# The first norm of a hybrid trunk: squares summed on TensorE, root spread by transpositions, first products in another order

## The chip, the cores and the metric

The kernel runs on one core of a Trainium2 chip. The metric is the device time of one execution in microseconds (us); the smaller the better. A core has TensorE (PE in the profile; PEld are its weight loads), VectorE (DVE), ScalarE (ACT), GpSimd (POOL) and SyncE (SP), which issues most of the loads. The four compute engines run their own instructions in order, and wait for each other by semaphores.

## The reference

The kernel computes two layers of a decoder trunk on one sequence of 1024 positions with 1024 channels. What matters here is the beginning: the first norm, its scale and shift, which come from the vector c, and the first product of the convolution module.

```python
def rms_norm(x, g):
    xf = x.astype(jnp.float32)
    y = xf * lax.rsqrt(jnp.mean(xf * xf, axis=-1, keepdims=True) + EPS)
    return (y * g.astype(jnp.float32)).astype(x.dtype)

def modulate(h, shift, scale):
    return h * (1.0 + scale[:, None, :]) + shift[:, None, :]

def reference(x, c, ada_w, ada_b, norm_mix_g, ...):
    c_act = jax.nn.silu(c)
    for i in range(DEPTH):
        mod = c_act @ ada_w[i] + ada_b[i]
        sh_m, sc_m, g_m, sh_f, sc_f, g_f = jnp.split(mod, N_ADA, axis=-1)
        h = modulate(rms_norm(x, norm_mix_g[i]), sh_m, sc_m)
        if i % N_MIXERS == 0:
            y = conformer_conv(h, ...)
        else:
            y = multiscale_pool(h, ...)
        x = x + (1.0 + g_m)[:, None, :] * y
        h = modulate(rms_norm(x, norm_ffn_g[i]), sh_f, sc_f)
        x = x + (1.0 + g_f)[:, None, :] * swiglu_ffn(h, ...)
    return rms_norm(x, final_g)
```

In the first layer `sh_m` and `sc_m` are dots of silu(c) with columns of `ada_w`; `conformer_conv` begins with `h @ w1`.

## The kernel before

Channels lie on the 128 partitions, positions along the free dimension. So x has eight channel tiles (KT = 8), and the sequence is worked in two chunks of 512 positions, A and B. All that the change touches is the opening for chunk A, the code of `trunk` from where `spread_c` is made to where the early weights of the next part are loaded, and `load_weight`.

The opening goes like this. SP issues loads in a fixed order (`load_next`): four transfers of x, each with two channel tiles, then `vecs` (all the small vectors), and then for each channel tile k a matrix `adaw` (two blocks of 128x1024: those rows of `ada_w` that give the shift and the scale of the tile's channels) and a weight `raw` (128x1024, the part of w1 for this channel tile and the first 2 x FIRST = 8 output tiles). TensorE spreads c over all partitions (the products named `c`), and ScalarE takes its SiLU (`cact`).

Of each channel tile the squares are taken, on VectorE for those in ON_DVE and on ScalarE for the others, and VectorE adds them up in `acc`. TensorE sums `acc` over the partitions: `mean_rsqrt` makes four products with `acc`'s 128x128 blocks as stationary operand and a column of `ones` (each 1/1024) as the moving one, into a bank named `var`. The function `rsqrt` takes the inverse root on VectorE in eight small operations on 128x4 elements (`col`, `var`). TensorE then spreads `col` over the partitions into the bank `rstd`, with `ident` as moving operand.

The loop over k (KT + 1 passes) then has, for each channel tile: two dots (`ada_dot`, a SCALAR_TENSOR_TENSOR of 128x1024 on VectorE that writes a column of `mod`), two small operations that make scale (`gains`) and shift (`mod`), then `t` = x times scale times rstd on VectorE, the high part of h on ScalarE (`h<-t,mod`), its low part on VectorE (`h<-t,mod,h`), and 24 products on TensorE: for each of the eight output tiles q (banks `first`), weight high x h high, weight high x h low, weight low x h high. A weight's high part is a CAST on ScalarE (`w<-raw`), its low part a subtraction (`w<-raw,w`), on VectorE for the first two (`own`) and on GpSimd for the others.

The order of TensorE's instructions is that of the code. On the other engines a scheduler chooses it from its own model of the times, bound by the manual dependences (`tc.add_manual_dep`), which keep an instruction behind another one of the same engine. After the opening the products `a` and `g` of the next output tiles begin, and pieces of work for VectorE and GpSimd are put beside them by a clock of planned costs.

The lines that set the order around the change are these:

```python
    ada_dot(w[:, 1], 0, 1, 0)
    tc.add_manual_dep(V_.last.ins, summed, edge, reason="behind the sums")
    rstd_p = now(mean_rsqrt(acc, A.n))
...
            for q in range(2 * FIRST):
                products(fb[q], wt, q, h_a[k - 1], k == 1, k == KT)
```

## Time and profile before

| | us |
|---|---|
| median of three runs | 1695.77 |
| lowest, highest | 1695.59, 1695.80 |
| the profiled execution | 1696.16 |
| its span, from the first to the last instruction | 1694.4 |
| TensorE busy in it | 1665.3 |
| VectorE busy in it | 1319.9 |

The profile is of one execution. Its page gives the busy time of each engine, the span in forty slices, the DMA queues, the chain of work that ended last and the costliest groups of instructions. Beside the page, the trace answers views of stretches: a timeline of instructions (start, length, engine, line, operation, output<-inputs, count, and in brackets the idle time before it with what ended it), groups by tile, and windows with busy time by engine. Names have no buffer numbers there. L149 and L126 are the lines of the helpers that issue a product and a vector operation, so one goes by the tiles' names. The whole opening lasts from 0 to 66 us of the span.

### The profile page before, as it was taken

The page shows a single profiled execution, that of the slowest core. Times are in us where ns is not written, and L with a number is a line of the kernel's source. Part 1 is how long each engine was busy: PE and PEld are TensorE (multiplying, and loading weights), DVE is VectorE, ACT ScalarE, POOL GpSimd, SP SyncE. Part 2 cuts the span into 40 slices and gives each one's busy share as a digit, 9 for nine tenths or more (in the row PEclk, how much of TensorE's full clock was granted, in tenths as well). Part 3 has the DMA queues.
Part 4 walks back from the last instruction along what each step waited for, and adds up shares of the span by engine and source line. Part 5 has one row for each costly group of instructions (what it writes and reads, how often), then busy time and mean ns, then how long its engine had stood idle before and what let it go on. Part 6 is the DMA issues. An engine that isn't in the chain of part 4 may idle for free.

```text
span 1694.4 us, 21271 instructions
## 1 busy us (share of the span) xinstructions
PE 1665.3 (98%) x7586; PEld 1356.4 (80%) x7586; DVE 1319.9 (78%) x1872; ACT 799.4 (47%) x1085; POOL 486.3 (29%) x566
## 2 busy tenths in 40 slices
PE   7999999999999999999999999999999999999997
PEld 5777777778887888888888888888888888888886
DVE  8889899899758887887665797848777677668657
ACT  3669686866546332333213336646422222234454
POOL 3587767796001111212110222100111111000013
PEclk9999999999999999999999999999999999999999
DMA  8858987828675788886878846877677776586564
GB/s 302 288 172 230 228 237 199 223 79 238 216 240 152 256 261 298 281 259 212 339 267 281 256 149 202 240 245 212 176 233 230 212 222 193 200 273 204 193 166 122
DMA packets 115820, 380.70 MB, mean 225 GB/s; under 512 B 12225, under 2 KB 14401, under 8 KB 115714
## 3 DMA queue, kind: packets, MB, share of 16 engines
q1 hardware_dynamic: 77888, 247.46, 41.3%
q0 software_dynamic: 36736, 130.83, 31.6%
q8 instruction: 60, 0.98, 0.2%
q10 hardware_dynamic: 1090, 1.05, 0.2%
q14 instruction: 46, 0.38, 0.1%
HBM read 311.92 MB, written 63.18 MB: 221 GB/s over the span
## 4 chain that ended last, share of the span: by engine, by line
PE 88%; DVE 5%; DMA 2%; ACT 2%; issue 2%; POOL 1%; DVEq 0%; SPq 0%; ACTq 0%; POOLq 0%
PE a L149 24%; PE dn L149 23%; PE e L149 13%; PE p L149 12%; PE y L149 6%; PE g L149 3%; PE first L149 3%; PE tap L149 2%; POOL pa L126 1%; PE ada L149 1%; DMA adaw<-in_adan_dram 1%; DVE t L126 1%; DVE x L126 1%; PE var L149 1%; DVE ca L126 0%
## 5 line engine op out<-in xcount | busy, mean ns | idle before, releaser
L126 ACT CAST w<-raw 128x1024 fp32r<-128x1024 f32 (+1 forms) x249 | 258.5, 1041 | 332.6 <-PE dn L149 98.6
L149 PE MATMUL dn<-g,w 128*128 128x512 f32 x1152 | 265.4, 391 | 2.3 <-DVE g L126 1.0
L149 PEld LDWEIGHTS dn<-g,w 128*128 128x128 f32 x1152 | 215.4, 188 | 48.7 <-DVE x L126 1.7
L126 DVE TENSOR_TENSOR w<-raw,w 128x1024 fp32r<-128x1024 f32 (+1 forms) x177 | 217.9, 1234 | 41.3 <-ACT w L126 40.8
L149 PE MATMUL a<-n,w 128*128 128x512 f32 x1056 | 247.7, 390 | 1.1 <-DVE n L126 0.7
L149 PE MATMUL p<-h,w 128*128 128x512 f32 x1056 | 244.2, 391 | 0.8 <-DVE h L126 0.6
L126 POOL TENSOR_TENSOR pa<-pa,pr 128x512 f32<-128x512 f32 x160 | 228.2, 1510 | 23.9 <-ACT pr L126 17.8
L149 PEld LDWEIGHTS a<-n,w 128*128 128x128 f32 x1056 | 197.9, 188 | 44.1 <-DVE n L126 2.2
L149 PEld LDWEIGHTS p<-h,w 128*128 128x128 f32 x1056 | 197.4, 188 | 43.7 <-DVE h L126 1.5
L149 PE MATMUL dn<-hi,w 128*128 128x512 f32 (+1 forms) x600 | 173.6, 373 | 0.4 <-DVE w L126 0.4
L126 DVE SCALAR_TENSOR_TENSOR ca<-u,vecs,ca 128x512 f32<-128x512 f32 x245 | 169.9, 748 | 0.5
L126 DVE SCALAR_TENSOR_TENSOR x<-dn,gains,x 128x512 f32<-128x512 f32 (+1 forms) x144 | 100.9, 732 | 35.9 <-PE dn L149 35.9
L149 PEld LDWEIGHTS dn<-hi,w 128*128 128x128 f32 x600 | 109.7, 188 | 20.4 <-DVE w L126 0.9
L149 PE MATMUL a<-t,w 128*128 128x512 f32 x528 | 123.6, 390 | 0.8 <-DVE w L126 0.8
L149 PE MATMUL e<-b,w 128*128 128x512 f32 x528 | 123.4, 389 | 0.6 <-DVE r L126 0.6
L149 PE MATMUL e<-t,w 128*128 128x512 f32 x528 | 123.2, 389 | 0.0
L126 ACT ACTIVATE pr<-u,vecs 128x512 f32<-128x512 f32 x160 | 108.3, 716 | 25.2 <-POOL pa L126 17.6
L1117 POOL DMA_DIRECT2D raw<-in_wgu_dram x41 | 36.3, 884 | 283.9 <-DVE k L126 100.7
L149 PEld LDWEIGHTS a<-t,w 128*128 128x128 f32 x528 | 99.1, 188 | 21.7 <-DVE w L126 1.2
L149 PEld LDWEIGHTS e<-b,w 128*128 128x128 f32 x528 | 99.1, 188 | 21.5 <-DVE r L126 1.1
L149 PEld LDWEIGHTS e<-t,w 128*128 128x128 f32 x528 | 99.2, 188 | 20.5
L149 PE MATMUL dn<-lo,w 128*128 128x512 f32 (+1 forms) x300 | 111.7, 372 | 0.0
(183 smaller groups left out, 2375.2 us busy)
## 6 DMA issues: line engine op xcount, KB each, us to landing
raw<-in_wgu_dram SPq DMA_DIRECT2D x132, 512.0 KB, 4.9
adaw<-in_ada_dram POOLq DMA_DIRECT2D x48, 512.0 KB, 7.4
raw<-in_wdn_dram SPq DMA_DIRECT2D x44, 512.0 KB, 7.9
raw<-in_wgu_dram POOLq DMA_DIRECT2D x41, 512.0 KB, 7.1
raw<-in_w_dram SPq DMA_DIRECT2D x36, 512.0 KB, 6.1
gd<-g POOLq DMA_DIRECT2D x36, 512.0 KB, 7.8
g<-gd SPq DMA_DIRECT2D x36, 512.0 KB, 5.8
kinds<-k POOLq DMA_DIRECT2D x33, 512.0 KB, 7.2
```

Source lines behind the costliest of these rows:

```text
L126: self.last = self.order(getattr(self.eng, name)(out, *args, **kw))
L149: last_mm[0] = nc.tensor.matmul(out, lhsT, rhs, start=start, stop=stop, skip_group_check=more).ins.name
L1117: d = order(nc.gpsimd.dma_start(w[i], wgu[l, fp, src], accum_op=ADD))
```

## The change

The squares are no longer added on VectorE. TensorE takes each of them as it comes: nine groups of four products into the bank `first_var`, the first with a constant tile `eps`, and the others with the squares of the eight channel tiles. Squares alternate between ScalarE and VectorE (ON_DVE is now 1, 3, 5, 7). The inverse root is taken as before, and `col` is spread by four transpositions (`turned`) in place of four products. The first matrix is loaded in two halves, the scale's half ahead of `vecs`; both of its dots stand behind the root. In the first channel tile the eight products of high with high parts come first, then those with h's low part, and then those with the weight's low part. The low parts of the first two weights stand behind t on VectorE, and the casts of the first four weights behind the previous h on ScalarE (`behind`). The SiLU of c's columns stands behind the last square.

```diff
--- before.py
+++ after.py
@@ -54,7 +54,7 @@
 DIAGS = 8
 LOAD = {"load": 4.0, "slow": 6.0, "next": 4.0, "dots": 4.0}
 
-ON_DVE = (1, 4)
+ON_DVE = (1, 3, 5, 7)
 AHEAD = 4
 RECENT = 6
 STRASSEN = (False, True)
@@ -362,6 +362,8 @@
     ones = cst.tile([P, P], F32, name="ones")
     V_.memset(ones, 1.0 / D)
     S_.activation(tmp.tile([P, 16], F32, tag="col0", name="first_act", bufs=1)[:, 0:1], ones[:, 0:1], AF.Silu)
+    eps = cst.tile([P, P], F32, name="eps")
+    V_.memset(eps, EPS_SUM)
     ident = cst.tile([P, P], F32, name="ident")
     make_identity(nc, ident)
     recip = cst.tile([P, PHALO], F32, name="recip")
@@ -485,12 +487,14 @@
         return mod[:, b : b + 1]
 
 
-    def load_weight(src, n=D, load=nc.sync.dma_start, summed=False, own=False):
+    def load_weight(src, n=D, load=nc.sync.dma_start, summed=False, own=False, behind=None):
         raw = raws.tile([P, D], F32, tag="raw", name=nm("raw"))[:, :n]
         dst = raw if len(src.shape) == 2 else raw.rearrange("p (a b) -> p a b", a=src.shape[1])
         load(dst, src)
         wt = wts.tile([P, 2, D], F32R, tag="w", name=nm("w"))
         S_.copy(wt[:, 0, :n], raw)
+        if behind:
+            tc.add_manual_dep(S_.last.ins, behind, edge, reason="behind the values before")
         if summed:
             S_.activation(wt[:, 1, :n], raw, AF.Copy, scale=-1.0)
             low = wt[:, 1, :n]
@@ -1680,49 +1684,58 @@
     spread_c = [bank("c") for _ in range(2)]
     for h in range(2):
         matmul(spread_c[h], ones[0:1, :], crow[:, h * 512 : h * 512 + 512], start=True, stop=True)
+    ada_m = ada.rearrange("(l j k) p d -> l k p j d", l=DEPTH, j=6)
+    first_w = wts.tile([P, 2, D], F32, tag="w", name=nm("adaw"))
+    load_next(first_w[:, 1], ada_m[0, 0][:, 1, :])
     load_next(vecs, vec)
-
-    squares = []
-
-    def square(k):
-        sq = temp(A.n) if k else temp(A.n, "acc", 2)
+    load_next(first_w[:, 0], ada_m[0, 0][:, 0, :])
+
+    first_var = bank("var")
+
+    def add_to_var(parts, first=False, last=False):
+        for i, part in enumerate(parts):
+            matmul(first_var[:, i : i + 1], part, ones[:, 0:1], start=first and i == 0, stop=last, more=True)
+
+    add_to_var([eps] * (A.n // P), True)
+    for k in range(KT):
+        sq = temp(A.n)
         if k in ON_DVE:
             V_.tensor_tensor(sq, x[0][k], x[0][k], op=MUL)
         else:
             S_.activation(sq, x[0][k], AF.Square)
-        squares.append(sq)
-
-    for k in range(KT):
-        square(k)
+            last_square = S_.last.ins.name
         if k == 2:
             for h in range(2):
                 S_.activation(cact[:, h * 512 : h * 512 + 512], spread_c[h], AF.Silu, scale=float(D))
-        if k > 1:
-            acc = squares[0]
-            V_.tensor_tensor(acc, acc, squares[k - 1], op=ADD)
-    V_.scalar_tensor_tensor(acc, squares[KT - 1], EPS_SUM, acc, op0=ADD, op1=ADD)
-    summed = V_.last.ins.name
+        add_to_var([sq[:, i * P : i * P + P] for i in range(A.n // P)], False, k == KT - 1)
     S_.activation(ccols[:, :, 0], V("c", 0, KT), AF.Silu)
     silu = S_.last.ins.name
+    tc.add_manual_dep(S_.last.ins, last_square, edge, reason="behind the squares")
     S_.activation(tmp.tile([P, 16], F32, tag="col0", name="second_act", bufs=1)[:, 0:1], ones[:, 0:1], AF.Sigmoid)
     tc.add_manual_dep(S_.last.ins, silu, edge, reason="the sigmoid's table early")
     scale_b = cst.tile([P, KT], F32, name="scale_b")
     G_.tensor_scalar(scale_b, V("ada_b", KT, KT), 1.0, None, op0=ADD)
-    ada_m = ada.rearrange("(l j k) p d -> l k p j d", l=DEPTH, j=6)
 
     def ada_pair(k):
         w = wts.tile([P, 2, D], F32, tag="w", name=nm("adaw"))
         load_next(w, ada_m[0, k][:, 0:2, :])
         return w
 
-    w = ada_pair(0)
+    w = first_w
+    count = A.n // P
+    cols = tmp.tile([P, 16], F32, tag="col1", name=nm("col"), bufs=1)
+    for _ in rsqrt(first_var[:, :count], cols[:, :count], first_var[:, 16 : 16 + count], cols[:, 8 : 8 + count], True):
+        pass
+    rstd_last = V_.last.ins.name
+    rstd_p = bank("rstd")
+    for i in range(count):
+        turned(rstd_p[:, i * P : (i + 1) * P], cols[:, i : i + 1].broadcast_to([P, P]))
     ada_dot(w[:, 1], 0, 1, 0)
-    tc.add_manual_dep(V_.last.ins, summed, edge, reason="behind the sums")
-    rstd_p = now(mean_rsqrt(acc, A.n))
-    rstd_last = V_.last.ins.name
+    tc.add_manual_dep(V_.last.ins, rstd_last, edge, reason="behind the root")
     first_t = bank("t")
     h_a = st["h", 0] = [pair("h0", "h") for _ in range(KT)]
     fb = [bank("first") for _ in range(BANKS)] + [spare_bank("first") for _ in range(2 * FIRST - BANKS)]
+    high_last = None
     for k in range(KT + 1):
         if k < KT:
             if k:
@@ -1735,28 +1748,35 @@
             dot = V_.last.ins.name
             V_.scalar_tensor_tensor(h_a[k - 1][1], t, mod[:, k - 1 : k], h_a[k - 1][0].bitcast(F32), op0=ADD, op1=SUB)
             low_last = V_.last.ins.name
-            if 1 < k < KT:
+            if 2 < k < KT:
                 tc.add_manual_dep(V_.last.ins, dot, edge, reason="the scalar engine's part takes that long")
-            for q in range(2 * FIRST):
-                products(fb[q], wt, q, h_a[k - 1], k == 1, k == KT)
+            elif k <= 2:
+                tc.add_manual_dep(V_.last.ins, weight_low, edge, reason="the scalar engine's part takes that long")
+            if k == 1:
+                for i, (wp, a) in enumerate(((0, 0), (0, 1), (1, 0))):
+                    for q in range(2 * FIRST):
+                        matmul(fb[q], wt[:, wp, q * P : (q + 1) * P], h_a[0][a], start=i == 0, stop=False)
+            else:
+                for q in range(2 * FIRST):
+                    products(fb[q], wt, q, h_a[k - 1], False, k == KT)
         if k < KT:
             ada_dot(w[:, 0], 0, 0, k)
-            dot2 = V_.last.ins.name
             tc.add_manual_dep(V_.last.ins, low_last if k else rstd_last, edge, reason="behind the first norm")
-            if k == 1:
+            if 1 <= k <= 2:
                 tc.add_manual_dep(dots[0], low_last, edge, reason="behind the first values")
             V_.tensor_scalar(scale_m[:, k : k + 1], mod[:, KT + k : KT + k + 1], scale_b[:, k : k + 1], V("norm_mix_g", k), op0=ADD, op1=MUL)
             V_.tensor_scalar(mod[:, k : k + 1], mod[:, k : k + 1], V("ada_b", k), None, op0=ADD)
             t = temp(A.n) if k else first_t
             V_.scalar_tensor_tensor(t, x[0][k], scale_m[:, k : k + 1], rstd_a if k else rstd_p, op0=MUL, op1=MUL)
             t_last = V_.last.ins.name
-            S_.activation(h_a[k][0], t, AF.Identity, bias=mod[:, k : k + 1])
+            before, high_last = high_last, S_.activation(h_a[k][0], t, AF.Identity, bias=mod[:, k : k + 1]).ins.name
             if k == 0:
                 rstd_a = temp(A.n, "ny", 2)
                 S_.copy(rstd_a, rstd_p)
-            wt = load_weight(w1f[k], 2 * FIRST * P, load_next, own=k < 2)
-            if k == 0:
-                tc.add_manual_dep(V_.last.ins, dot2, edge, reason="behind the root")
+            wt = load_weight(w1f[k], 2 * FIRST * P, load_next, own=k < 2, behind=before if k < 4 else None)
+            if k < 2:
+                tc.add_manual_dep(V_.last.ins, t_last, edge, reason="behind the first values")
+                weight_low = V_.last.ins.name
     st["T"] = {}
     for e in clock:
         clock[e] = max(clock.values())
```

What that does to the order of instructions shows at three places. The first is TensorE's opening, up to the spreading of the root. Before:

```order
L149 MATMUL c_266<-crow,ones 128x512
L149 MATMUL c_267<-crow,ones 128x512
L149 MATMUL var_304<-ones,acc_271 128x1 x4
L149 MATMUL rstd_318<-ident,col_309 128x128 x4
L149 MATMUL first_332<-h_324,w_349 128x512 x3
L149 MATMUL first_333<-h_324,w_349 128x512 x3
```

After (t are the squares):

```order
L149 MATMUL c_268<-crow,ones 128x512
L149 MATMUL c_269<-crow,ones 128x512
L149 MATMUL var_276<-ones,eps 128x1 x4
L149 MATMUL var_276<-ones,t_281 128x1 x4
L149 MATMUL var_276<-ones,t_287 128x1 x4
L149 MATMUL var_276<-ones,t_293 128x1 x4
L149 MATMUL var_276<-ones,t_301 128x1 x4
L149 MATMUL var_276<-ones,t_307 128x1 x4
L149 MATMUL var_276<-ones,t_313 128x1 x4
L149 MATMUL var_276<-ones,t_319 128x1 x4
L149 MATMUL var_276<-ones,t_325 128x1 x4
L157 MATMUL rstd_345<-ident,col_336 128x128 x4
```

One group of `var` products has become nine, all behind the products `c`; the spreading comes from another helper (L157, the transposition), and `first` follows as before.

The second place is VectorE round the root. Before, from the first dot to the second operation of the root:

```order
L126 SCALAR_TENSOR_TENSOR adaw_301,mod<-adaw_301,cact 128x1024
L126 TENSOR_SCALAR col_309<-var_304 128x4
L126 TENSOR_SCALAR gains<-mod,scale_b,vecs 128x1
L126 TENSOR_TENSOR var_304<-var_304,col_309 128x4
```

and from the last operation of the root on:

```order
L126 SCALAR_TENSOR_TENSOR col_309<-var_304,col_309 128x4
L126 SCALAR_TENSOR_TENSOR adaw_301,mod<-adaw_301,cact 128x1024
L126 TENSOR_TENSOR w_349<-raw_347,w_349 128x1024
L126 TENSOR_SCALAR mod<-mod,vecs 128x1
L126 SCALAR_TENSOR_TENSOR t_323<-x_79,gains,rstd_318 128x512
L126 SCALAR_TENSOR_TENSOR h_324<-t_323,mod,h_324 128x512
L126 SCALAR_TENSOR_TENSOR adaw_352,mod<-adaw_352,cact 128x1024 x2
```

After, from the last operation of the root (col) on:

```order
L126 SCALAR_TENSOR_TENSOR col_336<-var_276,col_336 128x4
L126 SCALAR_TENSOR_TENSOR adaw_272,mod<-adaw_272,cact 128x1024 x2
L126 TENSOR_SCALAR gains<-mod,scale_b,vecs 128x1
L126 TENSOR_SCALAR mod<-mod,vecs 128x1
L126 SCALAR_TENSOR_TENSOR t_351<-x_79,gains,rstd_345 128x512
L126 TENSOR_TENSOR w_377<-raw_375,w_377 128x1024
L126 SCALAR_TENSOR_TENSOR h_352<-t_351,mod,h_352 128x512
L126 SCALAR_TENSOR_TENSOR adaw_380,mod<-adaw_380,cact 128x1024 x2
L126 TENSOR_SCALAR gains<-mod,scale_b,vecs 128x1
L126 TENSOR_SCALAR mod<-mod,vecs 128x1
L126 SCALAR_TENSOR_TENSOR t_411<-x_79,gains,ny_373 128x512
L126 TENSOR_TENSOR w_416<-raw_414,w_416 128x1024
```

Of the norm, nothing but the four squares stands ahead of the root now. Both dots of the first matrix (adaw_272) stand behind it, and so does `gains`; the first weight's low part (w_377) has moved behind t, and the second weight's (w_416) from ahead of the second t to behind it.

The third place is SP, whose loads are in order. Before, from the last transfer of x:

```order
L181 DMA x_82<-in_xT_dram 128x1024
L181 DMA vecs<-in_vec_dram 128x448
L181 DMA adaw_301<-in_ada_dram 128x2x1024
L181 DMA raw_347<-in_w1f_dram 128x1024
L181 DMA adaw_352<-in_ada_dram 128x2x1024
```

After:

```order
L181 DMA x_82<-in_xT_dram 128x1024
L181 DMA adaw_272<-in_ada_dram 128x1024
L181 DMA vecs<-in_vec_dram 128x448
L181 DMA adaw_272<-in_ada_dram 128x1024
L181 DMA raw_375<-in_w1f_dram 128x1024
L181 DMA adaw_380<-in_ada_dram 128x2x1024
```

The first matrix has become two loads with `vecs` between them, and the first weight still stands behind both.

From the third channel tile on, the rows of VectorE, ScalarE, GpSimd and TensorE are those of before, apart from one square of chunk B on ScalarE behind the opening, which now stands ahead of a cast.

## The prediction

> **What bounds the kernel now.** I read the busy shares first, then the order of time of the opening, then the waits inside its steps.
>
> ```profile
> PE 1665.3 (98%) x7586; PEld 1356.4 (80%) x7586; DVE 1319.9 (78%) x1872; ACT 799.4 (47%) x1085; POOL 486.3 (29%) x566
> ```
>
> ```profile
> 3.06 3.75 PE L149 MATMUL c<-crow,ones 1*128 1x512 f32 x4 [3.06 <-DMA crow<-in_c_dram]
> 11.60 1.87 PE L149 MATMUL var<-ones,acc 128*128 128x1 f32 x8 [4.79 <-DVE acc L126]
> 15.52 2.05 PE L149 MATMUL rstd<-ident,col 128*128 128x128 f32 x8 [2.05 <-DVE col L126]
> 19.21 46.99 PE L149 MATMUL first<-h,w 128*128 128x512 f32 x192 [1.65 <-ACT h L126]
> 66.04 5.60 PE L149 MATMUL a<-h,w 128*128 128x512 f32 x24
> ...
> 91.95 1.05 PE L149 MATMUL var<-ones,acc 128*128 128x1 f32 x8
> ```
>
> TensorE is busy 98% of the span. Its timeline (start, length, what, count, idle time before it) shows pauses up to 19.21 us; from 66.04, where the products `a` of the next part begin, it hardly pauses. All that the change edits stands before that moment, and what the built orders show behind it is the same work in the same order on TensorE and GpSimd. So the question is: when can the products `a` begin?
>
> ```profile
> 4.05 0.33 PEld L149 LDWEIGHTS c<-crow,ones 1*128 1x128 f32 x1 [0.52 <-issue]
> ...
> 4.90 0.33 PEld L149 LDWEIGHTS c<-crow,ones 1*128 1x128 f32 x1 [0.52 <-issue]
> ...
> 9.39 1.15 ACT L126 ACTIVATE t<-x 128x512 f32<-128x512 f32 x2 [0.96 <-DMA x<-in_xT_dram]
> ...
> 10.85 0.69 DVE L126 SCALAR_TENSOR_TENSOR acc<-t,acc 128x512 f32<-128x512 f32 x1
> ...
> 12.49 1.23 DVE L126 SCALAR_TENSOR_TENSOR adaw<-adaw,cact 128x1024 f32<-128x1024 f32 x1 [0.94 <-DMA adaw<-in_ada_dram]
> ...
> 13.64 0.16 DVE L126 TENSOR_SCALAR col<-var 128x4 int32<-128x4 int32 x1
> ...
> 13.82 0.27 DVE L126 TENSOR_SCALAR gains<-mod,scale_b,vecs 128x1 f32<-128x1 f32 x1
> 14.01 0.16 DVE L126 TENSOR_TENSOR var<-var,col 128x4 f32<-128x4 f32 x1
> ...
> 15.21 0.16 DVE L126 SCALAR_TENSOR_TENSOR col<-var,col 128x4 f32<-128x4 f32 x1
> 15.29 1.22 DVE L126 SCALAR_TENSOR_TENSOR adaw<-adaw,cact 128x1024 f32<-128x1024 f32 x1
> ...
> 16.43 1.22 DVE L126 TENSOR_TENSOR w<-raw,w 128x1024 fp32r<-128x1024 f32 x1
> ...
> 17.69 0.75 DVE L126 SCALAR_TENSOR_TENSOR t<-x,gains,rstd 128x512 f32<-128x512 f32 x1
> 18.48 0.69 ACT L126 ACTIVATE h<-t,mod 128x512 fp32r<-128x512 f32 x1 [3.67 <-DVE t L126]
> ```
>
> Down these rows and TensorE's runs the chain of the opening: the last piece of x lands at 9.39, VectorE adds the last square at 10.85, TensorE sums over partitions at 11.60, VectorE takes the root from 13.64 to 15.37, then come the second dot, the low part of the weight, t, ScalarE's h, and the first product at 19.21. Then eight channel tiles follow, 24 products each. Who paces them? The same timeline further on, and TensorE's loads of the last tile:
>
> ```profile
> 22.15 1.22 DVE L126 TENSOR_TENSOR w<-raw,w 128x1024 fp32r<-128x1024 f32 x1
> ...
> 23.29 0.27 DVE L126 TENSOR_SCALAR gains<-mod,scale_b,vecs 128x1 f32<-128x1 f32 x1
> ...
> 23.59 0.75 DVE L126 SCALAR_TENSOR_TENSOR t<-x,gains,ny 128x512 f32<-128x512 f32 x1
> 24.26 1.22 DVE L126 SCALAR_TENSOR_TENSOR adaw<-adaw,cact 128x1024 f32<-128x1024 f32 x1
> ...
> 25.40 0.75 DVE L126 SCALAR_TENSOR_TENSOR h<-t,mod,h 128x512 fp32r<-128x512 f32 x1
> 26.07 1.22 DVE L126 SCALAR_TENSOR_TENSOR adaw<-adaw,cact 128x1024 f32<-128x1024 f32 x1
> 26.13 3.41 POOL L126 TENSOR_TENSOR w<-raw,w 128x1024 fp32r<-128x1024 f32 x1 [15.91 <-ACT w L126]
> ...
> 27.52 2.57 DVE L126 SCALAR_TENSOR_TENSOR t<-x,gains,ny 128x512 f32<-128x512 f32 x1
> ...
> 31.82 1.21 DVE L126 SCALAR_TENSOR_TENSOR adaw<-adaw,cact 128x1024 f32<-128x1024 f32 x1
> 31.87 3.42 POOL L126 TENSOR_TENSOR w<-raw,w 128x1024 fp32r<-128x1024 f32 x1 [2.33 <-ACT w L126]
> ...
> 33.27 2.56 DVE L126 SCALAR_TENSOR_TENSOR t<-x,gains,ny 128x512 f32<-128x512 f32 x1
> ```
>
> ```profile
> 60.69 5.09 PEld L149 LDWEIGHTS first<-h,w 128*128 128x128 f32 x23 [0.39 <-DVE h L126]
> ```
>
> VectorE does. From the third tile on, t starts every 5.75 us (27.52, 33.27). In that ring t does not end before GpSimd's product w has (26.13 + 3.41 = 29.54, t ends at 30.09): 0.75 us becomes 2.57. TensorE, quicker than that, waits for VectorE's h in each step, the last time at 60.69. So the end of this stage moves one for one with VectorE's third t, and the first product's own start (19.21) is not what ends last.
>
> **The change, part by part.** I count from R, the start of the root's last operation on VectorE. Before, R is 15.21, the third t ends at 30.09, R + 14.88.
>
> *The sums.* VectorE loses seven additions (0.69 each by the row at 10.85) and gets two squares more and one memset; all of it lies ahead of the root. TensorE gets nine groups (the constant, then eight squares) in place of one. One group is eight loads and products, by the row at 11.60. What do they cost?
>
> ```profile
> L149 PE MATMUL var<-ones,acc x96: 165/250/373, 11.6 to 1684.3; 128*128 128x1 f32 x96
> ```
>
> ```profile
> 20.00:21.00 1.00, 1.00 (x3) 1.00 0.22 86
> 21.00:22.00 1.00, 1.00 (x4) 1.00 0.00 0
> ...
> 23.00:24.00 1.00, 1.00 (x6) 1.00 0.49 127
> ```
>
> The first row gives one product's shortest, median and longest time in ns. At 11.60 the pitch is (1.87 - 0.37) / 7 = 0.214 us, at 91.95 it is (1.05 - 0.25) / 7 = 0.114: the same instruction at half and at full speed. The last rows (time, PE busy, products begun, granted clock) show when TensorE changes: after 19.21 it begins 3 or 4 products a microsecond, from 23 on 6. The clock column reads 1.00 throughout, so the opening must be read from the pitch. The rise came some 3.4 us after the products began; the `c` products, 3.75 us from 3.06, brought none by 11.60.
>
> 72 loads now stand in TensorE's queue behind `c`. Those four start 0.85 apart (4.05, 4.90), so the queue is free at 6.6. By then half of the squares exist, and with the last piece of x at 9.39 all do by about 10.2: the loads, not the squares, set the end. Slow throughout: 6.6 + 71 x 0.214 + 0.37 = 22.2. Fast throughout: 6.6 + 71 x 0.114 + 0.25 = 14.9. Both lie behind the 13.47 (11.60 + 1.87) of before. I take a rise between 3.4 us (what the first products needed) and twice that, the middle being 5.1, at 11.7: 24 slow loads to 11.74, then 47 x 0.114 + 0.25 = 5.6, so 17.35; with the two ends of that span, 16.5 and 18.2.
>
> *The root.* 13.64 stood 0.17 behind the sums; seven more operations followed by 15.21, of which `gains` between took 0.19 (13.82 to 14.01), and that goes. So R = sums' end + 0.17 + 1.57 - 0.19, or + 1.55: 18.9.
>
> *Behind the root* now stand both dots; before, one ran at 12.49, hidden behind the sums. VectorE idles meanwhile, so that cover is lost. The root is spread by four transpositions in place of four fp32 products (15.52, eight passes); both end under the dots, so nothing is gained or lost. From R: 0.08, two dots at 1.14 (15.29 to 16.43), gains and mod 0.30 (23.29 to 23.59): t at R + 2.66 (before 2.48). Then t 0.67 (23.59 to 24.26), the weight's low part 1.14 (22.15 to 23.29), h's low part 0.67 (25.40 to 26.07), two dots 2.28, gains and mod 0.30: second t at R + 7.72 (before R + 8.38, so 0.66 won). But the second weight's low part now stands behind it: 0.67 + 1.14 + 0.67 + 2.28 + 0.30 brings the third t to its start after 5.06. It ends 2.57 later if GpSimd's product comes behind the second dot, as now, or 2.27 + 0.75 later if it comes between the dots (31.87 + 3.42 ends 2.27 behind a dot begun at 31.82 and 1.2 long). So it ends at R + 15.35 to R + 15.8, against R + 14.88: 0.5 to 0.9 lost, I take 0.7.
>
> The Trainium skill, "SBUF — State Buffer", section "SBUF: two separate sides", says that VectorE with two SBUF inputs and GpSimd take one shared port pair in turn, for whole instructions. The 2.57 of t agrees; by that rule GpSimd slips in between the two dots, which gives the 0.9.
>
> *The rest.* High parts first lets eight products run before h's low part; it takes away the one gap behind the first product, but VectorE's ring ends later, so it is worth nothing. ScalarE's reordered casts and the last SiLU behind the squares lie in waits for t (3.67 at 18.48). SP issues one load more, and the first matrix comes in halves round `vecs`: the bytes ahead of the first weight are as many, and no load of before is what VectorE waits for after 12.49. The third and fifth matrices' buffers come free by VectorE as t does, about 2 us ahead of need. Zero for all of it, at most 0.5 either way.
>
> The sum: R moves from 15.21 to 18.9, 3.7; with 0.7, **4.4 us**. The profiled execution took 1696.16 (span 1694.4), 0.39 above the median of 1695.77; the difference is put on the median: **1700.2**. With the rise at 10.0 or 13.4 it is 3.6 or 5.2.
>
> **The rivals.** *TensorE never speeds up during the sums*, since they are nearly all loading and a product has one column. For it: no row shows such a stretch raising the pitch, and the 1.87 us at 11.60 did not. Against: they fill the queue as densely as any. Then sums end at 22.2, R = 23.7, 8.5 + 0.7 = 9.2: 1705.0.
>
> *It speeds up earlier*, because `c` counts as the beginning of the busy stretch: rise between 6.6 and 10.0, 2.0 to 3.6 us, middle 2.8: 1698.6. For it: no gap would lie between 3.06 and the sums' end. Against: `c` alone did not do it, with one row of the array.
>
> The Trainium skill, "TensorE: Matmul & The Clock Gate", Part 1, "What's actually happening", says that the clock doubles after a whole busy window of about 3.4 us which runs freely. By that rule this earlier rise is the one to expect if `c` counts as busy; the first products' 3.4 us agree, and no row shows which work counts.
>
> *The sums keep up with the squares*, the other side: last square at about 10.1, one fast group behind it, end at 11.2, R = 12.7, and with the 0.7 it is 1.8 faster: 1694.0. It decides from R = 14.5, a sums' end of 12.95, or a pitch of (12.95 - 0.25 - 6.6) / 71 = 0.086 us. The fastest row shows 0.114.
>
> **How the numbers follow.** Forecast 0.36, never 0.32, earlier 0.24, keeping up 0.08. A measurement of this kernel tells 0.2%, 3.4 us, from no change. Slower by more: 0.32, most of 0.36 and a little of 0.24, 0.66. Within: the rest of the earlier rise and most of the last rival, 0.32. Faster by more would need R 4.1 sooner, at 11.1, before the last square is summed: 0.02. The range runs from 1697.3, leaving out the last rival and the fastest corner of the earlier rise, to 1705.6, the slow case with 0.5 over.
>
> **What would show it.** Pitch of the small products (0.214 or 0.114) and where it changes; VectorE idle from about 10 us until the sums end; the first of the root near 17.5; both dots behind it; third t's end near 34.5; the last step's loads 4.4 later than 60.69, and `a` as much later than 66.04. Wrong if the sums end before 13 us, or if the steps stop repeating at 5.75.

## The result, and the profile after

The changed kernel takes 1709.71 us (median of five runs, 1709.32 to 1713.97) against 1695.80 (five runs): a ratio of 1.0083, 95% interval 1.0071 to 1.0094. It is 13.9 us slower, 9.5 above the forecast and 4 above the range. The profiled execution took 1709.71, 13.55 more than that of before.

The first lines are TensorE's timeline of the changed kernel (start, length, operation, count, idle time before it and what ended that).

```profile
2.26 3.75 PE L149 MATMUL c<-crow,ones 1*128 1x512 f32 x4 [2.26 <-DMA crow<-in_c_dram]
5.94 1.87 PE L149 MATMUL var<-ones,eps 128*128 128x1 f32 x8
7.66 13.79 PE L149 MATMUL var<-ones,t 128*128 128x1 f32 x64
23.20 1.09 PE L157 MATMUL rstd<-ident,col 128*128 128x128 f32 x4 [1.75 <-DVE col L126]
27.19 47.72 PE L149 MATMUL first<-h,w 128*128 128x512 f32 x192 [2.90 <-ACT h L126]
74.75 5.60 PE L149 MATMUL a<-h,w 128*128 128x512 f32 x24
...
100.66 0.64 PE L149 MATMUL ada<-adaw,ccols 128*32 128x256 f32 x8 [1.59 <-DMA adaw<-in_adan_dram]
101.23 1.05 PE L149 MATMUL var<-ones,acc 128*128 128x1 f32 x8
...
561.50 0.73 PE L149 MATMUL a<-t,w 128*128 128x512 f32 x2
564.22 6.90 PE L149 MATMUL a<-t,w 128*128 128x512 f32 x22 [1.99 <-DVE w L126]
```

The 64 products of the squares take (13.79 - 0.36) / 63 = 0.213 us each from the first to the last: 15.5 us of work without a gap (5.94 to 21.46) and no rise of speed. The products `a` begin 8.71 later than at 66.04. Next VectorE and GpSimd, same timeline:

```profile
21.49 0.16 DVE L126 TENSOR_SCALAR col<-var 128x4 int32<-128x4 int32 x1 [6.13 <-PE var L149]
...
22.90 0.16 DVE L126 SCALAR_TENSOR_TENSOR col<-var,col 128x4 f32<-128x4 f32 x1
22.98 1.22 DVE L126 SCALAR_TENSOR_TENSOR adaw<-adaw,cact 128x1024 f32<-128x1024 f32 x1
...
25.66 0.75 DVE L126 SCALAR_TENSOR_TENSOR t<-x,gains,rstd 128x512 f32<-128x512 f32 x1
...
30.79 0.75 DVE L126 SCALAR_TENSOR_TENSOR t<-x,gains,ny 128x512 f32<-128x512 f32 x1
...
33.33 3.39 POOL L126 TENSOR_TENSOR w<-raw,w 128x1024 fp32r<-128x1024 f32 x1 [22.18 <-ACT w L126]
...
34.40 3.40 DVE L126 SCALAR_TENSOR_TENSOR adaw<-adaw,cact 128x1024 f32<-128x1024 f32 x1
...
38.05 0.75 DVE L126 SCALAR_TENSOR_TENSOR t<-x,gains,ny 128x512 f32<-128x512 f32 x1
...
41.97 2.57 DVE L126 SCALAR_TENSOR_TENSOR t<-x,gains,ny 128x512 f32<-128x512 f32 x1
```

R, the root's last operation, is at 22.90. The third t ends at 38.80, R + 15.90: GpSimd's product came between the two dots, and the second of them took 3.40 us. From the fourth t on the steps are 5.75 apart as before.

The opening is 8.71 us. Where are the other five? TensorE's waits behind `a` give the places. In the timeline of before the two that grew most are these (the first row is SP's issue of the load that the second row waits for; the third waits for VectorE):

```profile
78.51 0.33 SPq L167 DMA_DIRECT2D adaw<-in_adan_dram  x1
...
91.38 0.64 PE L149 MATMUL ada<-adaw,ccols 128*32 128x256 f32 x8 [1.02 <-DMA adaw<-in_adan_dram]
...
553.34 5.28 PE L149 MATMUL a<-t,w 128*128 128x512 f32 x22 [0.76 <-DVE w L126]
```

The waits went from 1.02 to 1.59 and from 0.76 to 1.99. Behind the second stands this, in the windows of the changed kernel (time, length, TensorE busy, products begun, granted clock, DMA share, GB/s):

```profile
561.60:565.00 3.40, 1.41 (x5) 1.00 0.63 202
565.00:568.40 3.40, 3.40 (x9) 0.50 0.00 0
568.40:571.80 3.40, 3.40 (x16) 1.00 0.79 207
```

After the wait TensorE runs 3.41 us at half speed, 9 products where the next window has 16. From the first `a` to TensorE's last instruction the changed kernel takes 1625.71 us, before 1621.12: 4.59 more. TensorE is idle there, all its waits together, for 12.70 us against 10.28, 2.43 more; 3.41 us at half speed cost 1.71; 0.45 is left over. The five runs fit: the mean clock is 0.997, 0.996, 0.997, 0.995 and 0.994 at 1709.32, 1709.36, 1709.71, 1712.01 and 1713.97 us, and each 0.001 of it is one such half-speed window, 1.7 us.

So there are two questions: what the opening costs by its parts, and why more is lost behind it.

### The profile page after: what moved, and what is told of

The parts are those of the page before. It is cut to its first block, busy times and chain, and to the rows that moved or that the text cites. A ratio compares the mean times of both kernels' runs of the same rounds, so it can differ in the third digit from the quotient of the medians.

```text
span 1707.7 us, 21376 instructions
## 1 busy us (share of the span) xinstructions
PE 1680.8 (98%) x7646; PEld 1370.3 (80%) x7646; DVE 1317.4 (77%) x1868; ACT 799.6 (47%) x1083; POOL 489.8 (29%) x566
## 3 DMA queue, kind: packets, MB, share of 16 engines
q10 hardware_dynamic: 1090, 1.05, 0.2%
## 4 chain that ended last, share of the span: by engine, by line
PE 85%; DVE 6%; DMA 2%; issue 2%; ACT 1%; POOL 1%; DVEq 0%; ACTq 0%; POOLq 0%
PE a L149 23%; PE dn L149 21%; PE e L149 13%; PE p L149 12%; PE y L149 6%; PE g L149 3%; PE first L149 3%; PE tap L149 2%; DVE x L126 1%; POOL pa L126 1%; PE ada L149 1%; DMA adaw<-in_adan_dram 1%; DVE win L126 1%; DMA adaw<-in_ada_dram 1%; DVE t L126 1%
```

## The experiments

Each run is compared with the kernel before on the same chip. "Opening" is the start of the first `a` less 66.04, in the profiled execution; "behind" is the difference of the medians less the opening. The intervals reach 1.5 to 2.6 us to either side, so a "behind" near 2 says little alone.

**e1: half the products.** Each odd square is added to the even one on VectorE, and the pair is summed: 40 loads for 72.

```diff
+            V_.tensor_tensor(even, even, sq, op=ADD)
+            add_to_var([even[:, i * P : i * P + P] for i in range(A.n // P)], False, k == KT - 1)
```

> The changed kernel, but VectorE adds the squares in pairs, so TensorE takes five groups of one-column products, 40 loads in place of 72; the built order is otherwise that of the changed kernel everywhere. Theory of the slow pitch (TensorE stays at half speed through such products, whatever their number): 32 loads x 0.213 us = 6.8 us less, sums end at 14.6 us instead of 21.5, the products a begin at about 67.9 instead of 74.75. Rival (the opening is late for another reason, the lost cover of the dots or the casts): a begins within 2 us of 74.75. For the 4.6 us that the changed kernel loses behind the opening: if they follow from the length of the delay, the time is 1697 to 1699 us; if they belong to other parts of the change, about 1702.

1702.75 us, ratio 1.0032 (1.0022 to 1.0041), 5.9 above. TensorE's timeline:

```profile
7.68 6.96 PE L149 MATMUL var<-ones,t 128*128 128x1 f32 x32
...
67.94 5.60 PE L149 MATMUL a<-h,w 128*128 128x512 f32 x24
```

Half the products take half the time, still 0.213 apart, and 6.8 of the 8.7 us go. The opening is 1.90, behind it 4.0 are lost.

**e2: the same 72 products, 120 columns wide** in place of one, the first column used. Only the moving columns differ (and some instructions behind the opening change places).

```diff
-            matmul(first_var[:, i : i + 1], part, ones[:, 0:1], start=first and i == 0, stop=last, more=True)
+            matmul(first_var[:, i * P : i * P + WIDE], part, ones[:, 0:WIDE], start=first and i == 0, stop=last, more=True)
```

> The changed kernel with 120 moving columns of ones in each variance product in place of one (the sum stands in 120 equal columns, the first is used); the number of loads, 72, stays. If TensorE's speed follows from columns streamed through the array, it rises some 3.4 to 7 us into them, the pitch goes from 0.213 to about 0.115, sums end at 15 to 18 us and the products a begin 3.5 to 6.5 us earlier than 74.75. If such short products never raise it, or the loads alone decide, the pitch stays at 0.213 and a begins at 74 to 75. The order of VectorE and ScalarE behind the opening differs a little from the changed kernel's, so the whole time is not compared closer than 3 us.

1703.61, ratio 1.0044 (1.0031 to 1.0058), 6.8 above. Timeline and windows:

```profile
7.94 8.55 PE L150 MATMUL var<-ones,t 128*128 128x120 f32 x64
...
69.80 5.60 PE L150 MATMUL a<-h,w 128*128 128x512 f32 x24
```

```profile
7.00:10.50 3.50, 3.50 (x19) 1.00 1.02 390
10.50:13.90 3.40, 3.40 (x32) 1.00 1.02 418
...
20.80:24.20 3.40, 1.97 (x5) 0.50 0.00 0
```

From 10.5 on 32 products a window begin where 19 did: the speed rose at 10.5 us, and wider products finished 5.0 us sooner than narrow ones (16.49 against 21.46). So what held the speed down was not the queue, nor the loads, which are the same: one-column products did not count as work. While VectorE took the root and the dots the speed fell again (window from 20.80). Opening 3.76, behind it 3.0.

**e3: sums on VectorE again,** with the first dot ahead of the root again and ON_DVE as before. The transpositions, the halved load, the high parts first and the casts of the change are kept.

```diff
+        if k > 1:
+            acc = squares[0]
+            V_.tensor_tensor(acc, acc, squares[k - 1], op=ADD)
+    for i in range(A.n // P):
+        matmul(first_var[:, i : i + 1], acc[:, i * P : i * P + P], ones[:, 0:1], start=True, stop=True)
```

> The changed kernel with the squares added on VectorE again and one group of variance products, and the first dot again ahead of the root; the halved load, the transpositions, the high parts first and the order of low parts and casts stay. If the sums on TensorE and the lost cover are the whole cost of the opening: root's last operation at about 15.0, third t ends at 29.3 to 29.8 (before 30.09), products a at 65.3 to 65.8, time 1694.9 to 1695.7. If one of the kept parts costs, a begins later than 66.5 and the time is above 1697.

1701.40, ratio 1.0025 (1.0015 to 1.0035), 4.6 above, yet:

```profile
66.02 2.20 PE L149 MATMUL a<-h,w 128*128 128x512 f32 x9
```

The opening is as long as before (-0.02), where 0.2 to 0.7 less had been expected: the sums, with the dot that lost its cover, are its whole cost, and the other edits neither gain nor lose there. The 4.6 us lie behind it.

**e4: the kernel before with five more groups** of products with zeros behind its sum.

```diff
+        for e in range(extra):
+            for i in range(count):
+                matmul(b[:, i : i + 1], zeros, ones[:, 0:1], start=False, stop=e == extra - 1, more=True)
```

> The kernel before with five more groups of variance products (with zeros, 40 loads) behind the one it has, nothing else of the change: a pure delay of the root. Slow pitch: 40 x 0.213 = 8.5 us, products a at 74.6. If a delay of that length passes through as it is: 1704.3 us. If the loss behind the opening comes from the length of the delay: 1707 to 1710. If TensorE speeds up in the 48 products, the delay is 5 to 7 us.

1706.90, ratio 1.0054 (1.0039 to 1.0069), 10.1 above.

```profile
13.24 8.67 PE L150 MATMUL var<-ones,zeros 128*128 128x1 f32 x40
...
73.22 5.60 PE L150 MATMUL a<-h,w 128*128 128x512 f32 x24
```

40 products in 8.67, again slow to the end; 7.18 us of it reach `a`. Behind it 2.9, with instructions on VectorE, ScalarE and GpSimd in other places there.

**e5 to e8: is it the delay?** Theory A: any shift of the tuned order costs more behind it. Theory C: parts of the change do. e5 is the changed kernel again. e6 and e7 are the kernel before with 3 and 6 GpSimd products that meet VectorE's additions; the order of all else stays. e8 shortens a step in place of lengthening one.

```diff
+    for _ in range(HELD):
+        nc.gpsimd.tensor_tensor(h_a[KT - 1][0], squares[4], squares[4], op=MUL)
```

```diff
-            wt = load_weight(w1f[k], 2 * FIRST * P, load_next, own=k < 2)
+            wt = load_weight(w1f[k], 2 * FIRST * P, load_next, own=k < 3)
```

> The changed kernel as it is, beside the kernel before and the three runs below on one chip. Its time was 13.9 us above the kernel before's, and only 8.7 us of that stand at the first product behind the opening (74.75 for 66.04). Theory A (the order behind the opening is tuned to the opening's end; any shift of it moves loads against their use, and a few waits grow): 12 to 15 us above the kernel before. Theory B (the rest belonged to the chip or the moment of that timing): 8 to 10 us above.

> The kernel before, with three products of 128x512 on GpSimd into a tile that is overwritten later; the order of the instructions is that of the kernel before on every engine but GpSimd. VectorE's additions meet them, so the root comes later by perhaps 2 to 5 us (each GpSimd product is put at 1.7 us, half of the 3.41 us of a 128x1024 subtraction). Theory A (shift alone): the time rises by the shift of the first a product and 2 to 5 us more. Theory C (what is lost behind the opening belongs to parts of the change, such as its loads, its casts or the squares' order): the time rises by the shift alone, within 1 us.

> As the run before with six products: a shift of perhaps 5 to 9 us, near the 8.7 us of the change, and none of the change's parts. Theory A: the shift and 2 to 5 us more. Theory C: the shift alone, within 1 us.

> The kernel before with the third tile's low part of the weight on VectorE instead of GpSimd, one instruction moved and no other order changed. The third t (2.57 us beside GpSimd's 3.41 us, 0.75 us without) should end about 1.8 us earlier, and the first a product come up to 1.8 us earlier if the steps keep their 5.75 us pitch; if the fourth step is bounded by its load instead, 0 to 0.5 us. Theory A (any shift costs, of either sign): the time ends 0 to 3 us above the kernel before although the opening is shorter. Theory C: below the kernel before by the shift.

e5: 1712.62, ratio 1.0093 (1.0079 to 1.0107), 15.7 above, opening 8.78: it is no accident of one chip, theory B falls. But its five executions lie between 1706.56 and 1714.35, and the profiled one, the fastest, lost only 1.8 behind its opening: what is lost there varies from one execution to the next. e6: 5.2 above (1.0028, 1.0017 to 1.0040) with an opening of 2.02; e7: 2.1 above (1.0012, 1.0003 to 1.0021) with 2.50, where 5 to 9 had been expected. The two contradict each other, 3.2 and -0.4 behind. In e6's profile stands

```profile
95.06 1.08 PE L150 MATMUL ada<-adaw,ccols 128*32 128x256 f32 x8 [2.67 <-DMA adaw<-in_adan_dram]
```

and 6.83 us at half speed behind it, in e7's a wait of 0.84 and none. e8: 0.2 above (1.0000, 0.9991 to 1.0009), opening 0.11:

```profile
28.87 0.74 DVE L126 SCALAR_TENSOR_TENSOR t<-x,gains,ny 128x512 f32<-128x512 f32 x1
...
35.87 1.23 DVE L126 SCALAR_TENSOR_TENSOR adaw<-adaw,cact 128x1024 f32<-128x1024 f32 x1 [0.52 <-DMA adaw<-in_ada_dram]
```

The third t ends at 29.61, 0.48 sooner than at 30.09 though it no longer meets GpSimd, and two steps on a dot waits for its load. So this edit gains nothing at `a`: the loads stand close behind.

**e9 and e10: the fourth `ada` product later,** in the changed kernel and in the one before.

```diff
             yield "load"
+            if i == 3 and j == 2:
+                yield "load"
```

> The changed kernel with the fourth ada product and those behind it one group of 24 products later, so that its load (13.4 us in the changed kernel, 12.8 us in the kernel before, for 12.5 us between issue and use) has landed; this moves parts of the order behind it too. Theory D (what is lost behind the opening is waits for loads, at this ada product and at the a product near 564 us, each with 3.41 us windows at half speed once the wait passes about 2 us): the wait of 1.6 to 1.8 us at the fourth ada product goes, and the median comes down from 1712.6 by 2 to 5 us, with higher mean clocks. Rival C (the loss belongs to other parts of the change): no less than 1711.

> The same edit in the kernel before, whose wait there is 1.02 us. Theory D: 1 us less than the kernel before if the reordered part costs nothing, with a smaller spread of its times; if the later order costs more than the wait, 0 to 2 us more, and then the run of the changed kernel with this edit is read against it.

e9: 1713.81, ratio 1.0098 (1.0083 to 1.0114), 16.3 above; e10: 1699.50, ratio 1.0015 (1.0006 to 1.0024), 2.0 above. The expectation for e9 failed. The wait near 100 did go, but in the moved order waits of 1.76 and 2.11 us arose at 164 and 192 with 3.41 us at half speed behind each. Moving the place only moved the loss.

**e11 and e12: larger shifts,** by 3 and 5 GpSimd products of 128x1024 during the additions.

```diff
+    spare = block("h0", "h")
+    for _ in range(HELD):
+        nc.gpsimd.tensor_tensor(spare, xp[0][1], xp[0][1], op=MUL)
```

> The kernel before with three GpSimd products of 128x1024 (each put at 3.4 us) into a tile that is overwritten later, from the arrival of the second pair of x tiles on; no other order changes. VectorE's squares and additions meet them: the root later by perhaps 4 to 8 us. Theory A (behind the opening more is lost because everything is shifted): the median rises by the shift and 3 us or more. Theory D (what is lost behind are waits for loads and half-speed windows, which do not follow from the shift's size): the shift and 0 to 3 us, and in the profiled run the rest is the growth of TensorE's waits behind the first a product plus half of the half-speed time, within 1 us. Theory C (the change's own parts): the shift within 1 us.

> The same with five products, a shift of perhaps 6 to 10 us, about the 8.7 us of the changed kernel, with the order of the kernel before and none of the change's parts. Theory A: 13 us or more above the kernel before for a shift near 9, as the changed kernel shows. Theory C: the shift within 1 us. Theory D: between the two, with the same sum of waits and half-speed time.

e11: 1701.25, ratio 1.0034 (1.0022 to 1.0046), 4.4 above, opening 4.36. e12: 1703.15, ratio 1.0040 (1.0028 to 1.0052), 6.3 above, opening 7.82. e12's timeline and windows (its profiled execution is the slowest of five, 1706.76, and lost 2.7 behind):

```profile
11.32 6.88 POOL L1698 TENSOR_TENSOR h<-x 128x1024 fp32r<-128x1024 f32 x3
11.88 6.86 DVE L127 TENSOR_TENSOR acc<-acc,t 128x512 f32<-128x512 f32 x3
...
73.86 5.60 PE L150 MATMUL a<-h,w 128*128 128x512 f32 x24
...
99.09 0.64 PE L150 MATMUL ada<-adaw,ccols 128*32 128x256 f32 x8 [0.90 <-DMA adaw<-in_adan_dram]
99.66 1.05 PE L150 MATMUL var<-ones,acc 128*128 128x1 f32 x8
```

```profile
98.00:101.40 3.40, 2.50 (x21) 1.00 1.07 360
101.40:104.80 3.40, 3.40 (x10) 0.50 1.02 314
```

Three additions took 6.86 us beside GpSimd. Nearly the whole delay of the change, without its parts, passes on at 6.3 of 7.8 in the median: theory A falls.

**e13 and e14: the load more in SP's queue,** taken out of the changed kernel (its first matrix whole), and put into the kernel before.

```diff
-    load_next(first_w[:, 1], ada_m[0, 0][:, 1, :])
     load_next(vecs, vec)
-    load_next(first_w[:, 0], ada_m[0, 0][:, 0, :])
+    load_next(first_w, ada_m[0, 0][:, 0:2, :])
```

```diff
     load_next(vecs, vec)
+    load_next(more, vec[0:1, 0:64])
```

> The changed kernel with its first ada load whole again, behind the vectors' load, as the kernel before has it: one load fewer in SP's queue, and the order of every other instruction that of the changed kernel. The first dots stand behind the root at 22.9 us, so the opening should stay 8.7 us longer. Theory E (one load more in SP's queue puts every later load out of step with the others in the queues, and the waits behind the opening grow by that): what is lost behind the opening falls from 5 to 7 us (medians) to at most 2, the time is 8 to 11 us above the kernel before. Theory F (the rest of the change, such as one square that ScalarE now runs ahead of a cast, or chance): still 13 to 16 us above.

> The kernel before with one more load, 256 bytes of the vectors into a tile that nothing reads, behind the vectors' load in SP's queue; every other instruction stands where it stood. Theory E: 2 to 5 us above the kernel before, though the first a product comes within 0.5 us of 66.04. Theory F: within 1 us of the kernel before.

e13: 1708.80, ratio 1.0073 (1.0060 to 1.0086), 11.4 above. e14: 1696.21, ratio 0.9993 (0.9985 to 1.0002), 1.2 below. One small load more costs nothing by itself. e13 fell between the expectations, and its interval meets those of the changed kernel: that the halved load costs something there is not shown.

**e15 and e16: two places on ScalarE.** The built orders of before and after behind the opening differ in this alone: a square of chunk B (`acc<-x`) stands ahead of a cast and the negation of the same weight, and the fourth gate (`t<-first`) ahead of the next cast. In ScalarE's timeline of before, then of the changed kernel (`w<-raw` as CAST is the cast, as ACTIVATE the negation):

```profile
64.17 1.03 ACT L126 CAST w<-raw 128x1024 fp32r<-128x1024 f32 x1
...
66.06 0.59 ACT L126 ACTIVATE acc<-x 128x512 f32<-128x512 f32 x1
...
67.15 1.04 ACT L126 CAST w<-raw 128x1024 fp32r<-128x1024 f32 x1
...
69.05 0.68 ACT L126 ACTIVATE t<-first,vecs 128x512 f32<-128x512 f32 x1
```

```profile
72.88 0.59 ACT L126 ACTIVATE acc<-x 128x512 f32<-128x512 f32 x1
73.40 1.04 ACT L126 CAST w<-raw 128x1024 fp32r<-128x1024 f32 x1
...
75.29 1.26 ACT L126 ACTIVATE t<-first,vecs 128x512 f32<-128x512 f32 x2
76.43 1.05 ACT L126 CAST w<-raw 128x1024 fp32r<-128x1024 f32 x1
```

Against the first `a` (66.04 and 74.75) both casts come 0.5 to 0.6 us later. e15 puts the two so in the kernel before, e16 in e12's.

```diff
+                for ins in st["first_cast"]:
+                    tc.add_manual_dep(ins, S_.last.ins.name, edge, reason="ahead of the first cast")
...
+                for ins in (cast, S_.last.ins):
+                    tc.add_manual_dep(ins, st["fourth"], edge, reason="behind the fourth gate")
```

> The kernel before with the one thing that the built order of the changed kernel has otherwise behind its opening: on ScalarE one square of the second chunk stands ahead of the cast and the negation of a weight tile, and a gate ahead of the next cast, so that each cast comes 0.5 us later and with it the next loads. Theory G (this swap makes the loads meet others and the waits behind the opening grow): 2 to 5 us above the kernel before, with the first a product at 66.0 as before. Theory H (the swap is harmless): within 1 us.

> The same swap in the kernel of e12 (five wide GpSimd products, a shift of 7.8 us and 6.3 us in the median): the order of every instruction behind the opening is then that of the changed kernel, without its loads and products. Theory G: 9 to 12 us above the kernel before. Theory H: 5 to 8 us; then what the changed kernel loses behind its opening comes from neither its order nor the length of its delay alone.

e15: 1699.12, ratio 1.0011 (1.0002 to 1.0020), 2.3 above with the opening at -0.16. e16: 1707.04, ratio 1.0059 (1.0046 to 1.0072), 10.2 above: 3.9 more than e12, though its opening is 0.14 shorter. e15's timeline (the load's issue by SP, then its product) and windows:

```profile
78.35 0.33 SPq L167 DMA_DIRECT2D adaw<-in_adan_dram  x1
...
92.15 0.79 PE L149 MATMUL ada<-adaw,ccols 128*32 128x256 f32 x8 [1.95 <-DMA adaw<-in_adan_dram]
```

```profile
89.10:92.50 3.40, 1.45 (x13) 1.00 1.05 298
92.50:95.90 3.40, 3.40 (x19) 0.50 1.05 323
95.90:99.30 3.40, 3.40 (x9) 0.50 1.05 306
```

The load, issued at 78.35, had landed when the product began at 92.15, after 13.8 us; in before it is issued at 78.51 and used at 91.38, after 12.9. Without a wait some 12 us lie between the two. 0.93 us more of wait and 6.83 us at half speed (3.4 lost) follow. The load is issued 12.47 us behind the first `a` in all these kernels. From issue to landing it takes 13.3 to 13.8 us in the profiles of all six with the swapped order, and 12.6 to 13.3 in six of the seven with the order of before (e6: 14.5). All DMA engines are busy (share 1.05), so a cast that gives its buffer back 0.5 us later may change what the load shares them with; that is not shown. The medians put the swap at 2.3 us (interval 0.3 to 3.4) in e15 and 3.9 between e12 and e16, whose intervals against the kernel before just meet (4.8 to 8.8 and 7.8 to 12.2): that it costs something is well supported, how much is not settled.

**e17 and e18: the swap taken out** of the changed kernel, and out of e13's. The built order does not go back to that of before: instructions on VectorE, ScalarE and GpSimd move too, between 79 and 210 us. The edit also frees some later copies of weights on ScalarE from a dependence, which moves nothing behind that.

```diff
+                tc.add_manual_dep(S_.last.ins, st["negs"][0].name, edge, reason="behind the first cast")
...
+                tc.add_manual_dep(st["fourth"], S_.last.ins.name, edge, reason="behind the second cast")
```

> The changed kernel with the square held behind the first cast pair and the fourth gate behind the second, as the kernel before has them on ScalarE. The order of some later taps, products on GpSimd and activations moves with it (between the first convolutions), so it is no pure undoing. Theory G: the 14 to 16 us above the kernel before fall by 2 to 4 us, to 10 to 13. Theory H: 13 us or more.

> The same with the first ada load whole (e13's edit): behind the opening neither the swap nor the load more. Theory G: the opening's 8.7 us and 0 to 2 us, 8 to 11 us above the kernel before. Theory H: 11 us or more, as e13.

e17: 1708.59, ratio 1.0072 (1.0059 to 1.0084), 11.9 above, as theory G has it, though its interval meets that of the changed kernel. e18: 1710.97, ratio 1.0079 (1.0066 to 1.0093), 14.2 above, which theory G does not have: there the wait at the fourth `ada` is 1.99 again. Opening and behind, all runs together:

| behind `a` the order is | kernels: opening / behind, us |
|---|---|
| that of before | e6 2.0 / 3.2; e7 2.5 / -0.4; e8 0.1 / 0.1; e11 4.4 / 0.1; e12 7.8 / -1.5; e14 -0.1 / -1.1 |
| that of the changed kernel | the changed kernel 8.7 / 5.2; e5 8.8 / 6.9; e1 1.9 / 4.0; e13 8.7 / 2.7; e15 -0.2 / 2.4; e16 7.7 / 2.5 |
| another | e2 3.8 / 3.0; e3 0.0 / 4.6; e4 7.2 / 2.9; e9 8.7 / 7.6; e10 -0.1 / 2.1; e17 8.8 / 3.1; e18 8.9 / 5.3 |

In the medians five of six with the order of before lose nothing behind the opening, whatever the shift; with any other order every one loses 2 to 8 us. Of the six with the changed kernel's order, the three that load the first matrix in halves lose 4.0 to 6.9, the three that load it whole 2.4 to 2.7; with intervals of some 2 us that points at the halved load and does not show it. In the profiled executions the loss behind is TensorE's waits, for loads and for other engines, and half speed: the growth of the waits plus half of the half-speed time leaves 0.0 to 1.1 us over or short in each of the runs. The same wait can cost a half-speed stretch or not: e14's 1.49 us at the fourth `ada` did, the changed kernel's 1.59 did not.

## Why the prediction was wrong

*The sums* were the step that failed first. It took the rise of TensorE's speed at 11.7 us; the products keep 0.213 to the end. The rival "TensorE never speeds up", for the reason it gave (nearly all loading, one column), is what happened, and its 9.2 us stands against 8.71. The earlier rise did not come either. In the sum, the term of 3.7 for R measured 7.69 (15.21 to 22.90). The parts of the rival: sums' end 22.2, measured 21.46, since `c` began 0.8 earlier; root + 1.55, measured 1.44; the third t's loss 0.7, measured 1.02. With R from each trace, R + 15.90 - 30.09 gives the opening of e1 (R 16.08) as 1.89 and of e2 (R 17.93) as 3.74; measured 1.90 and 3.76.

*Behind the root* the prediction was nearly right: both dots uncovered, t at R + 2.76 (for 2.66), the second at R + 7.89 (for 7.72), GpSimd between the dots, the second of the two cases that it left open. The Trainium skill, "SBUF — State Buffer", section "SBUF: two separate sides", has VectorE and GpSimd take a shared port pair by whole instructions; the 3.40 us of that dot agree, and so do three additions in 6.86 us in e12. That case's 0.9 was nearer to the 1.02 than the 0.7 taken.

*The steps at 5.75* and the passing of the delay to `a` were right, as was zero for the other edits in the opening (e3).

*"From 66.04 it hardly pauses"* was the second failure. The text looked at the order on TensorE and GpSimd, found it the same, and priced what lies behind at nothing. ScalarE's order was not the same: the part on the change names the square that moved, not the gate, and gives it no price. "Hardly pauses" hid a wait of 1.02 us at a load that lands too late already. The changed kernel lost 5 to 7 us there in the median. The medians of e15 and e16 put 2.3 to 3.9 of it to the swap on ScalarE. What the rest is stays open: the shift alone lost nothing (e12), but chance in how loads meet, the halved first load (e13) and the shift together with the swap were not told apart, and e18 lost 5.3 with both parts out but with a third order. Nor is it shown by which other transfer the load is slowed.

## What to carry to other kernels

Don't put a sum of single-column products on the path in the hope that TensorE speeds up on them: price them at the slow pitch. Wider products do bring the speed up, but even so the opening of e2 was 3.76 us longer than before. When a tuned kernel's opening is changed, compare the built order on every engine to the end, ScalarE's too: here two instructions that moved by half a microsecond went with 2 to 4 us. And a wait of 1 us at a load, read as "hardly pauses", is a warning that the load has no slack, and that TensorE's speed behind it depends on it.

## What had not been expected of the hardware

One-column products count as no work for TensorE's speed: 72 of them without a gap did not raise it, while the same at 120 columns had raised it by 10.5 us. Nor do they keep it up. e12's window 98.00 to 101.40 is busy for 2.50 us, of which 1.05 are one-column products; 1.45 are left, and the speed fell. In e5, at the same place,

```profile
98.10:101.50 3.40, 1.57 (x13) 1.00 1.06 392
101.50:104.90 3.40, 3.40 (x23) 1.00 1.03 261
```

1.57 us without any such products kept it. The changed kernel's 1.41 and e15's 1.45 lost it. So the edge lies near 1.5 us of work in 3.41, blurred by the modelled ends: one window of 1.64 in e9 lost it too, and one of 1.37 near the end of e15 (2.93 less 1.56 of one-column products) kept it.

The Trainium skill, "TensorE: Matmul & The Clock Gate", section "What's actually happening", has the clock follow a window of 3413 ns that runs freely; the stretches here agree, 3.41 or 6.83 us long. Its section "Why this matters for your kernels" asks for no idle gaps over about 3 us; here 0.90 us beside one-column products, and 1.95 alone, were enough.
